# A sliding-window copy: batch 0 moved from the staged to the direct path, with larger transfers on two of the three DMA rings

## The chip, the cores and the metric

The kernel runs on one core of a Trainium2 chip. The metric is the device time of one execution in microseconds (us); three runs of the kernel before are shown, and their median is the time before. One execution was also taken by the hardware profiler; its span (first to last instruction on the core) is a little shorter than its time.

## The reference: what is computed

The input `x` has 32 batches of 4096 rows of 256 float32 values. Each batch is cut into windows of 64 rows that start every 32 rows, so that each window overlaps the next by half, and there are 127 windows in a batch. Nothing is calculated; the work is a copy in which nearly every input row is written twice.

```python
n_windows = (length - window_size) // stride + 1     # 127
for i in range(n_windows):
    start = i * stride
    result[:, i] = x[:, start:start + window_size].copy()
```

A block is 32 rows of 256 values, 32 KB (32,768 bytes). A batch is 128 blocks, 4.19 MB. A window is two neighbouring blocks, 64 KB, and the output of a batch is 127 windows, 8.32 MB. All outputs together are 266.3 MB.

## The kernel before, in words

All work is done by DMAs. There is no matmul and no arithmetic, and the engines' instruction streams only issue transfers and wait for semaphores. Two kinds of path carry the data.

**Staged batches.** Twelve batches (1, 4, 7, ... 28, then 30, then 0; line 134) are loaded into on-chip memory (SBUF) by `Copier.load` (L59, L60) as a tile of 128 partitions, one block each, and written out twice by `Copier.store` (L65, L72): once with every block as the first half of its window (`half` 0), and once as the second half (`half` 1). Each DMA of 128 rows is cut into pieces of 16,384 bytes. A staged batch so costs 4.19 MB in and 8.39 MB out. `Staging.run` (L109) issues these on ScalarE's ring (`ring_s`, called ACT here): six loads, the stores of these six, the next six loads, and the stores of those. There are six buffers, so a second-round load waits until its buffer is stored (L91).

A store of all 128 blocks writes one row too many: block 127 as a first half lies in window 127, which does not exist and is window 0 of the next batch; block 0 as a second half lies in the last window of the batch before. These spilled rows are wrong there, and the true windows have to be written after them. The last staged batch alone is stored without spilling, by four DMAs of 112, 15, 15 and 112 rows (L97 to L100), which count on a semaphore of their own, `last`. `spilled` (L139) is the list of the other eleven.

**Direct batches.** The other 20 batches are copied from DRAM to DRAM by `Copier.windows` (L42, L48), on SyncE's ring (`ring_d`, called SP). Each batch is seven jobs of 16 windows (1 MB each, L171 to L182). A job is issued either as one DMA of whole windows, or split into two DMAs of half-windows, one for each half. Either way its data go in pieces of 32,768 bytes. Which jobs are split is set by a fraction that is counted up at L174: `share += 12 if at < loads else 9`, and a job is split when the sum reaches 12. `turns` adds 4 for a split job and 3 for a whole one, which are the packets that one DMA engine handles for it: two data packets and one completion packet for each of its DMAs. `at` compares the turns so far with those of six loads (`6 * 17`) and their stores (`6 * 34`), so it tells whether the ACT ring is in a round of loads or of stores.

**Remainders.** Seven jobs of 16 cover 112 of 127 windows. The 15 windows left of each direct batch are those that lie beside a staged neighbour where there is one (`first`, L144, and `rest_parts`, L147), so that they are written after the neighbour's spilled rows. Batch 29 has a spilling neighbour on both sides and gets two parts, of 8 and 7 windows. The remainders are issued on GpSimd's software ring (`ring_r`, called POOL, L186 to L192). It first waits for `near`, which the third-last direct job sets (`todo == 3`, L179 and L182), and then, batch by batch in the order of their last staged neighbour, for that neighbour's stores (`wait_stored`, L190, with the wait itself at L107). The remainders take their piece size in turn from `PIECES`: 32,768 and 16,384.

At the end SP waits for the direct jobs, the remainders and the last staged batch (L193 to L195).

The queues in the profile are: q1 = SP's ring, q10 = ACT's ring, q0 = the software ring of POOL. All three feed the same 16 DMA engines.

Of the kernel before, what the change touches and what calls it, by code (L numbers as in the profile page):

```python
# [6 lines left out]


DIRECT, IN, OUT = 32768, 16384, 16384
PIECES = (32768, 16384,)  # L10


class Copier:
# [105 lines left out]
@with_exitstack  # L119
def kernel(  # L120
    ctx: ExitStack,
    tc: tile.TileContext,
    x: bass.AP,
    window_size: bass.AP,
    stride: bass.AP,
    out: bass.AP,
):
    nc = tc.nc
    W, S = int(window_size), int(stride)
    B, L, D = x.shape  # L130
    n_win = (L - W) // S + 1
    assert out.shape == (B, n_win, W, D)
    c = Copier(nc, tc, x, out, B, L, D, W, S, n_win)
    staged = [*range(1, B - 3, 3), B - 2, 0]
    direct = [b for b in range(B) if b not in staged]
    pool = ctx.enter_context(tc.tile_pool(name="xb", bufs=1))
    st = Staging(c, pool, x.dtype, staged, 6)
    ring_d, ring_s = nc.sync, nc.scalar
    spilled = staged[:-1]  # L139

    waits = {b: [g for g, n in enumerate(spilled) if abs(n - b) == 1] for b in direct}
    per, loads, stores = 6, 6 * 17, 34

    def first(b):  # L144
        return 0 if b - 1 not in spilled else 8 if len(waits[b]) == 2 else 15

    def rest_parts(b):  # L147
        if len(waits[b]) == 2:
            return [(0, 8), (120, 7)]
        return [(0 if b - 1 in spilled else 112, 15)]  # L150

    soft = tc.alloc_semaphore("soft")
    soft_total = 0

    near = tc.alloc_semaphore("near")

    def mark(dma):
        dma.then_inc(near, 16)

    def count_soft(dma):  # L160
        nonlocal soft_total
        dma.then_inc(soft, 16)
        soft_total += 16

    with tc.tile_critical():  # L165
        st.run(ring_s)

        turns = share = 0
        rests = []
        todo = 7 * len(direct)  # L170
        for b in direct:  # L171
            for j in range(7):
                at = turns % (loads + per * stores)
                share += 12 if at < loads else 9  # L174
                if share >= 12:
                    share -= 12
                    turns += 4
                    c.windows(ring_d, b, first(b) + 16 * j, 16, 0)
                    c.windows(ring_d, b, first(b) + 16 * j, 16, 1, count=mark if todo == 3 else None)  # L179
                else:  # L180
                    turns += 3
                    c.windows(ring_d, b, first(b) + 16 * j, 16, count=mark if todo == 3 else None)  # L182
                todo -= 1
            rests.append(b)

        ring_r = nc.gpsimd  # L186
        ring_r.wait_ge(near, 16)
        for i, b in enumerate(sorted(rests, key=lambda b: max(waits[b], default=0))):
            for g in waits[b]:
                st.wait_stored(ring_r, g)  # L190
            for w, n in rest_parts(b):
                c.windows(ring_r, b, w, n, None, PIECES[i % 2], count_soft)  # L192
        ring_d.wait_ge(c.done, c.total)  # L193
        ring_d.wait_ge(soft, soft_total)
        ring_d.wait_ge(c.last, c.last_total)  # L195
# [35 lines left out]
```

## Time and profile before

| What | Value |
|---|---|
| Time, median of 3 runs (lowest to highest) | 752.54 us (752.53 to 753.82) |
| Profiled execution: time | 752.54 us |
| Profiled execution: span | 750.8 us |
| Bytes moved by the DMA engines | 317.43 MB, 423 GB/s over the span |
| ACT ring (q10) | 9,818 packets, 150.93 MB |
| SP ring (q1) | 8,608 packets, 146.82 MB |
| Software ring (q0) | 1,328 packets, 19.66 MB |
| DMAs on SP | 236 of 512 KB, 22 of 1,024 KB |
| DMAs on ACT | 12 loads and 22 stores of 4,096 KB; 2 stores of 3,584 KB and 2 of 480 KB |
| DMAs on POOL | 19 of 960 KB, 1 of 512 KB, 1 of 448 KB |

A queue's line gives its packets (short completion packets included), its bytes, and the time that its packets took as a share of 16 engines over the span: 47.4% on q10 means 0.474 x 16 x 750.8 us of engine time. A DMA from SBUF to DRAM or back touches the DRAM once for each byte, a DMA from DRAM to DRAM twice, so the DRAM's traffic is larger than what the engines move.

### The profile page before, as it was taken

What the parts mean: (1) busy time and instruction counts of PE and PEld (TensorE: products, weight loads), DVE (VectorE), ACT (ScalarE), POOL (GpSimd) and SP (SyncE); (2) the same over time, 40 slices, a digit from 0 to 9 for tenths busy, and PEclk for the clock granted to TensorE, in tenths of its full rate; (3) what the DMA queues carried; (4) which work ended last, traced back from release to release, by engine and by line L of the source; (5) the groups of instructions that cost most, each with busy time, mean ns of one, the idle gap of its engine ahead of it and who ended that gap; (6) DMA issues with size and microseconds to landing.
All of it is one profiled execution on the core that took longest, in us unless ns stands there. A gap on an engine that the chain in (4) does not pass through costs nothing.

```text
span 750.8 us, 372 instructions
## 1 busy us (share of the span) xinstructions
POOL 12.2 (2%) x25
## 2 busy tenths in 40 slices
POOL 0000000000000000000000000000000000410000
DMA  9999999999999999999999999999999999999995
GB/s 377 433 428 433 432 431 424 430 428 433 437 423 433 433 430 443 423 432 429 423 425 431 430 433 433 432 433 429 428 436 432 429 431 436 430 427 430 417 394 220
DMA packets 19756, 317.43 MB, mean 423 GB/s; under 512 B 5162, under 2 KB 5162, under 8 KB 5162
## 3 DMA queue, kind: packets, MB, share of 16 engines
q10 hardware_dynamic: 9818, 150.93, 47.4%
q1 hardware_dynamic: 8608, 146.82, 45.6%
q0 software_dynamic: 1328, 19.66, 6.1%
q14 instruction: 2, 0.02, 0.0%
HBM read 216.79 MB, written 267.06 MB: 644 GB/s over the span
## 4 chain that ended last, share of the span: by engine, by line
another core or an unknown queue 92%; POOL 2%; issue 0%; POOLq 0%; SPq 0%
POOL out_dram L48 2%; POOLq L107 0%; POOLq L226 0%; SPq L165 0%
## 5 line engine op out<-in xcount | busy, mean ns | idle before, releaser
L48 POOL DMA_DIRECT2D out_dram<-in_x_dram x21 | 12.0, 577 | 692.7 <-DMA out_dram<-in_x_dram 648.5
L212 POOL MEMSET const-float32-0.0<- 128x1 f32 x1 | 0.1, 98 | 0.2 <-issue 0.2
L212 POOL MEMSET const-bfloat16-1.0<- 128x1 bf16 x1 | 0.1, 101 | 0.0
L212 POOL MEMSET const-float32-1.0<- 128x1 f32 x1 | 0.1, 98 | 0.0
L212 POOL MEMSET const-uint8-127<- 128x1 uint8 x1 | 0.1, 98 | 0.0
## 6 DMA issues: line engine op xcount, KB each, us to landing
out_dram<-in_x_dram SPq DMA_DIRECT2D x236, 512.0 KB, 87.5
out_dram<-xb ACTq DMA_DIRECT2D x22, 4096.0 KB, 128.6
xb<-in_x_dram ACTq DMA_DIRECT2D x12, 4096.0 KB, 119.9
out_dram<-in_x_dram SPq DMA_DIRECT2D x22, 1024.0 KB, 89.2
out_dram<-in_x_dram POOLq DMA_DIRECT2D x19, 960.0 KB, 44.3
out_dram<-xb ACTq DMA_DIRECT2D x2, 3584.0 KB, 112.3
out_dram<-xb ACTq DMA_DIRECT2D x2, 480.0 KB, 96.2
out_dram<-in_x_dram POOLq DMA_DIRECT2D x1, 512.0 KB, 36.6
```

Of the source, the lines that this page charges most:

```text
L48: q.dma_start(out=self.oap((b * self.nw + w0) * 2 * blk + off, [[2 * blk, n], [1, size]]), in_=bass.AP(self.x.tensor, self.x.offset + (b * ...
L212: nc = _bacc.Bacc("TRN2", target_bir_lowering=False, num_devices=1)
```

## The change

Batch 0 is taken off the staged list, and nothing is put in its place: 11 batches are staged and 21 are direct. Batch 30 is now the last staged one, so it is stored by the four DMAs that don't spill, and the neighbours 29 and 31 no longer wait for it; batch 29's remainder becomes one part of 15 windows. The share of split jobs becomes 9 of 12 in rounds of loads and 3 of 12 in rounds of stores, from 12 and 9. All remainders use pieces of 32,768 bytes.

```diff
-PIECES = (32768, 16384,)
+PIECES = (32768,)
...
-    staged = [*range(1, B - 3, 3), B - 2, 0]
+    staged = [*range(1, B - 3, 3), B - 2]
     direct = [b for b in range(B) if b not in staged]
...
                 at = turns % (loads + per * stores)
-                share += 12 if at < loads else 9
+                share += 9 if at < loads else 3
                 if share >= 12:
...
             for w, n in rest_parts(b):
-                c.windows(ring_r, b, w, n, None, PIECES[i % 2], count_soft)
+                c.windows(ring_r, b, w, n, None, PIECES[i % 1], count_soft)
```

In DMAs: ACT issues 11 loads instead of 12, 20 full stores instead of 22, and the same four of the last batch. SP issues 64 split jobs and 83 whole ones (128 DMAs of 512 KB and 83 of 1,024 KB) instead of 118 and 22. POOL issues 21 DMAs of 15 windows, each as 15 rows of two pieces, instead of 21 of three sizes.

## Prediction

> **What bounds the kernel now.** I read the page's strip of 40 slices first, then its queues, then the same queues in stretches.
>
> ```profile
> span 750.8 us, 372 instructions
> ...
> DMA  9999999999999999999999999999999999999995
> GB/s 377 433 428 433 432 431 424 430 428 433 437 423 433 433 430 443 423 432 429 423 425 431 430 433 433 432 433 429 428 436 432 429 431 436 430 427 430 417 394 220
> DMA packets 19756, 317.43 MB, mean 423 GB/s; under 512 B 5162, under 2 KB 5162, under 8 KB 5162
> ...
> q10 hardware_dynamic: 9818, 150.93, 47.4%
> q1 hardware_dynamic: 8608, 146.82, 45.6%
> q0 software_dynamic: 1328, 19.66, 6.1%
> ...
> HBM read 216.79 MB, written 267.06 MB: 644 GB/s over the span
> ```
>
> All 16 DMA engines are busy in every slice but the last, and the shares of the three rings add to 99.1%. The rate stands near 430 GB/s from the second slice to the third-last. So nothing but the engines' own time bounds the kernel: a wait that leaves the rings full costs nothing, and a byte taken off the rings is time taken off. (The chain of waits says only "another core or an unknown queue 92%", which is this same DMA time.)
>
> Is it the engines, or the DRAM behind them? A stretch in which rings have other shares tells.
>
> ```profile
> DMA packets 2664, 43.33 MB, mean 433 GB/s; under 512 B 717, under 2 KB 717, under 8 KB 717
> ## 3 DMA queue, kind: packets, MB, share of 16 engines
> q1 hardware_dynamic: 1335, 22.87, 53.4%
> q10 hardware_dynamic: 1328, 20.45, 47.7%
> ```
>
> These are 100 to 200 us. DRAM traffic there is 2 x 22.87 + 20.45 = 66.2 MB in 100 us, 662 GB/s, at 433 GB/s moved. In 660 to 700 us (8.62 MB on q10, 8.60 on q0, by the same view) it is 646 GB/s, at 431 moved. What the engines move doesn't fall when the DRAM carries more. The engines are the bound, as far as this trace reaches, which is 662. The same view shows **the turn order**: 1,335 packets of q1 and 1,328 of q10. An engine serves two full rings in turn, one packet each, and a completion packet takes a turn like any other. So the ring with larger packets gets more of the time.
>
> **Price of a byte on each ring.** Engine time by bytes, from the queue lines:
> - q10: 0.474 x 16 x 750.8 = 5,694 engine-us for 150.93 MB: 26.5 GB/s for one engine, 618 ns for a 16 KB packet with its share of completions.
> - q1: 0.456 x 16 x 750.8 = 5,478 for 146.82 MB: 26.8 GB/s, 1,223 ns for 32 KB.
> - q0: 0.061 x 16 x 750.8 = 733 for 19.66 MB: 26.8 GB/s.
>
> A byte from DRAM to DRAM so costs no more than one between SBUF and DRAM. A staged batch moves 4.19 + 8.39 MB, a direct one 8.32 MB.
>
> **The change, part by part.**
>
> 1. *Batch 0 leaves the staged list.* q10 after: 11 loads x 4.194 + 20 stores x 4.194 + the last batch's 254 rows, 8.32 = 138.35 MB, 12.58 less. At 26.5 GB/s that is -474.7 engine-us. q1 after: 147 jobs x 1.0486 = 154.14 MB, +7.34, or +273.9 at 26.8. q0: 21 x 15 windows = 20.64 MB, +0.98, or +36.6. Sum -164.2 engine-us, over 16 engines **-10.3 us**. Second way: the total falls by 4.295 MB (317.43 to 313.13); the stretches from 100 to 700 us moved 258.5 MB, 430.9 GB/s, so **-10.0 us**. I take -10.1.
>
> 2. *Fewer split jobs on SP.* Bytes and packet sizes stay; one DMA fewer for each job that is now whole. The completions on an engine go from 258 to 211. They are tiny (the price in 1 holds them): 0 to -0.5 us. What this does change is the turns: SP's ring needs 64 x 4 + 83 x 3 = 505 on each engine, from 118 x 4 + 22 x 3 = 538, so it carries more bytes in fewer turns.
>
> 3. *Larger pieces on the software ring.* The price of a byte was equal on q0 and q1, so 0 by itself; ten of 20 remainders had 16 KB pieces, and at q10's price against q1's (1%) of 9.8 MB the bound is 0 to 0.2 us. In turns: ten DMAs of 3 and ten of 5, 80 x 15/16 = 75 for an engine, become 21 x 3 x 15/16 = 59.
>
> 4. *Do the rings still end together?* ACT's turns: a 128-row DMA is 16 packets and a completion, 17; the last four stores are 15 + 3 + 3 + 15 = 36. Before 12 x 17 + 22 x 17 + 36 = 614, after 31 x 17 + 36 = 563. When SP is through, ACT has 614 - 538 = 76 turns left before, against 75 of q0; after, 563 - 505 = 58 against 59. The balance is kept. It also matters little: if one ring dries up, the engine gives all its time to the other.
>
> 5. *POOL's waits.* `near` is set two jobs before SP's end. Check of the count on before: a turn of q1 is 5,478/8,608 = 636 ns, of q10 5,694/9,818 = 580; 538 x 1.216 = 654, and with 2 us of start SP ends at 656, two split jobs (8 turns, 9.7 us) after `near`: 647.
>
> ```profile
> 648.99 9.74 POOL L48 DMA_DIRECT2D out_dram<-in_x_dram  x17 [648.54 <-DMA out_dram<-in_x_dram]
> 663.00 0.58 POOL L48 DMA_DIRECT2D out_dram<-in_x_dram  x1 [4.27 <-DMA out_dram<-xb]
> 703.44 1.70 POOL L48 DMA_DIRECT2D out_dram<-in_x_dram  x3 [39.86 <-DMA out_dram<-xb]
> ```
>
> The timeline has POOL going at 648.5, and the last wait, for a spilling batch's stores, over at 703.4; the count gives 76 - 36 = 40 turns of (580 + 611) after 656, 704. So it can be trusted for after: SP's turn is 154.14 MB / 26.8 / 16 = 359.5 us / 505 = 712 ns; it ends at 505 x 1.292 + 2 = 654, `near` lands about 646. Batch 28, the last that spills, is stored 22 turns of (580 + 812) later, at 685. Until then POOL holds back two remainders (27 and 29); behind them in POOL's stream is only the end. The 19 others keep q0 full for 57 turns, to about 654 + 57 x 1.39 = 733. The wait has 48 us of cover. If the cover were gone, two remainders would run alone after the rest, 2 x 2.4 us and a start of about 5.
>
> 6. *Loads in the second round.* Five loads instead of six lie ahead of the first store that waits for one of them. While that wait lasts ACT's ring holds four loads of 17 turns, over 80 us of work, so it doesn't dry up: 0.
>
> 7. *The tail.* At the end the engines don't stop together.
>
> ```profile
> DMA  9949939829658466134031222020010000000000
> ...
> DMA packets 269, 2.95 MB, mean 184 GB/s; under 512 B 117, under 2 KB 117, under 8 KB 117
> ...
> q0 software_dynamic: 216, 2.31, 33.9%
> q10 hardware_dynamic: 53, 0.64, 9.6%
> ```
>
> In 735 to 751 us the 2.95 MB would need 6.8 us at full rate; the last packets end in the 31st of 40 slices, near 747.5. About 3.5 us are the end of the program, and about 5 are spread between the engines. The strip falls from 700 us on (417, 394), while the last staged batch's 112- and 15-row stores run: the packet records show q10 packets of 1 to 4 us there instead of 0.61, 38 engine-us over the usual in all, 2.4 us for each engine, unevenly. These four stores remain, for batch 30. I take their cost and the spread as unchanged: 0. The bounds are -5 us (no spread) and +5 (twice the spread).
>
> **Sum:** 750.8 - 10.1 = 740.7 us of span. The profiled execution took 752.5, 1.7 over its span, and equals the median of the runs. **Forecast 742.4 us**, -1.35%.
>
> **A rule that speaks against it.** The change trades 4.19 MB of loads for direct reads: DRAM traffic goes from 483.9 to 487.9 MB. Measured is 644 GB/s over the span and 662 in a stretch. The Trainium skill (HBM Reference, Specifications (TRN2)) gives about 716 GB/s for a domain and about 358 as one core's part. By the 358 the added 4.06 MB would be an estimated +11 us, the wrong way; but the 644 of this trace already refutes it for this run. By the 716, 487.9 MB would be an estimated 681 us, which still leaves the engines as the bound.
>
> **Rivals.**
> - *The DRAM becomes the bound; slower.* In rounds of stores SP's ring will get 750/(750 + 580) = 56% of an engine's time (three whole jobs to a split one: 13 turns, 8 packets of 1,223 ns), so the DRAM carries 1.56 x 431 = 674 GB/s, 2% over what the trace shows. For it: at 369 us the records have all 16 engines start a direct packet within 1.3 us, and these take 1.31 to 1.54 us instead of 1.21. Against: only some 1% of direct packets were so stretched, and the engines then fall out of step. Price: held at 644 GB/s of DRAM, 487.9 MB need 758 us of span, **759 us**. It decides when the DRAM can't hold 650 GB/s in the mean, or when about 49 of an engine's 294 direct packets take 0.2 us more (49 x 0.208 = 10).
> - *Partly so:* stretched packets as in 350 to 400 us (10.6 engine-us over the usual in 50 us) all through would be 740 x 10.6 / 50 / 16 = 9.8 us: **752 us**, no change.
> - *The tail eats half:* the larger last packets and another hand of uneven stores double the spread, +5: **747.5 us**. The records give single engines up to 5 us more than the mean there, which speaks for some luck in it either way.
> - *The change doesn't keep the rings balanced* (POOL late, a ring dry): 5 to 10 us lost, **750 us**. Against it stand the counts of 4 and 5.
>
> **Chances.** Forecast within a few us 0.74, tail 0.10, balance lost 0.04, partly DRAM-bound 0.05, DRAM-bound 0.07. What a measurement can tell from no change is 0.2%, 1.5 us. Faster (under 751.0) 0.87, same 0.05, slower 0.08. Range: down to 738.5 (a spread smaller by 4 us), up to 748 (the tail's 747.5); what lies out of it is about 0.17.
>
> **What would show it.** q10 at 138.35 MB, q1 at 154.14, q0 at 20.64; the rate near 430 in the slices; 26.5 to 26.8 GB/s of each ring's engine time. POOL waiting for `near` until about 646 and for the last stores until about 685. A rate under 428 in the middle slices, with q1's price over 1,223 ns, is the DRAM. A rate of 430 with more than 16 us of falling strip is the tail.

## The result, and the profile after

The changed kernel took **745.38 us** (median of 4 runs, 745.27 to 745.96) against 752.6 us of the kernel before on the same chip: ratio 0.990, 95% interval 0.9885 to 0.9919. The forecast was 742.4, the range 738.5 to 748. So the direction held, the bytes and the balance of the rings came out nearly as counted, and about 3 us of the 10 are missing.

These are the lines of the page of the changed kernel that answer to those of before: the strip, the queues, and the DRAM's traffic.

```profile
span 743.5 us, 321 instructions
...
DMA  8999999999999999999999999999999999999995
GB/s 368 431 430 427 426 436 436 423 440 420 431 432 425 427 438 420 435 427 421 439 423 408 431 434 432 434 424 433 427 437 429 430 425 437 421 435 432 414 420 191
DMA packets 18092, 313.16 MB, mean 421 GB/s; under 512 B 4312, under 2 KB 4312, under 8 KB 4312
...
q1 hardware_dynamic: 8080, 154.15, 48.5%
q10 hardware_dynamic: 9002, 138.35, 43.8%
q0 software_dynamic: 1008, 20.65, 6.8%
...
HBM read 220.92 MB, written 266.99 MB: 656 GB/s over the span
```

The bytes are those of the count: 138.35, 154.15 and 20.65 MB. The three shares still add to 99.1%, so the engines were as full as before. Engine time by ring, by the prediction's own sum (one engine-us is one engine busy for 1 us; 16 of them are 1 us of the kernel):

| Ring | predicted, engine-us | measured | price of a byte, one engine |
|---|---|---|---|
| q10 | 5,694 - 475 = 5,219 | 0.438 x 16 x 743.5 = 5,210 | 26.55 GB/s (before 26.5) |
| q1 | 5,478 + 274 = 5,752 | 0.485 x 16 x 743.5 = 5,770 | 26.7 (26.8) |
| q0 | 733 + 37 = 770 | 0.068 x 16 x 743.5 = 809 | 25.5 (26.8) |
| sum | 11,741 | 11,789 | |

Against before's 11,905 that is -116 engine-us, or -7.3 us on 16 engines, and the span fell by just this, from 750.8 to 743.5. So the loss isn't in engines that stood idle: the same bytes took 48 engine-us more than by the old prices, 3.0 us, and most of it stands on q0. (A share is rounded to 0.1%, 12 engine-us; the packet records give 5,212, 5,775 and 806 for the three rings.)

The timeline of POOL shows the waits near where the count had put them (646 and 685 us were predicted; the first is 5 us late).

```profile
651.85 11.05 POOL L48 DMA_DIRECT2D out_dram<-in_x_dram  x19 [651.41 <-DMA out_dram<-in_x_dram]
685.76 1.16 POOL L48 DMA_DIRECT2D out_dram<-in_x_dram  x2 [22.86 <-DMA out_dram<-xb]
```

Where the bytes became dearer is seen in stretches. Here is 200 to 400 us, nearly all a round of stores, first of the kernel before, then of the changed one (packets, MB and share of the engines by queue).

```profile
DMA packets 5246, 85.94 MB, mean 430 GB/s; under 512 B 1392, under 2 KB 1392, under 8 KB 1392
...
q1 hardware_dynamic: 2623, 45.59, 53.3%
q10 hardware_dynamic: 2623, 40.35, 47.2%
```

```profile
DMA packets 4817, 85.63 MB, mean 428 GB/s; under 512 B 1072, under 2 KB 1072, under 8 KB 1072
...
q1 hardware_dynamic: 2409, 48.53, 57.1%
q10 hardware_dynamic: 2408, 37.09, 43.5%
```

Turns still go one to one, and q1 has the larger share that was meant. The DRAM's traffic rose from 2 x 45.59 + 40.35 = 131.5 MB (658 GB/s) to 134.2 (671 GB/s), and the engines moved 0.3 MB less in spite of fewer completions. The end shows it plainly. This is the changed kernel from 720 to 735 us, when ACT's ring has nearly run out:

```profile
DMA packets 290, 5.42 MB, mean 362 GB/s; under 512 B 104, under 2 KB 104, under 8 KB 104
...
q0 software_dynamic: 234, 4.75, 85.6%
q10 hardware_dynamic: 56, 0.67, 12.3%
```

The engines are 97.9% busy and move only 362 GB/s; the DRAM carries 2 x 4.75 + 0.67 = 10.17 MB in 15 us, 678 GB/s. That led to the **theory**: the DRAM holds no more than some 660 to 680 GB/s, and the change asks for more wherever direct packets take more than their mean share. The main **rival**: the engines are the only bound, and the 3 us are luck in the tail.

The packet records give sizes, as engine time over the usual 0.611 us for 16 KB and 1.213 us for 32 KB. For q1 it grew from 9 to 39 engine-us, for q0 from 2 to 38; for q10 it grew from 19 to 39 up to 650 us and fell from 39 to 9 after that. By time, all rings together: from 28 to 78 up to 650 us, in the rounds, and from 41 to 47 after that. So the rounds cost 3 us, and what q0 lost at the end ACT's ring nearly gave back.

### The profile page after: what moved, and what is told of

The parts are those of the page before. It is cut to its first block, busy times and chain, and to the rows that moved or that the text cites. A ratio compares the mean times of both kernels' runs of the same rounds, so it can differ in the third digit from the quotient of the medians.

```text
span 743.5 us, 321 instructions
## 1 busy us (share of the span) xinstructions
POOL 12.4 (2%) x25
## 3 DMA queue, kind: packets, MB, share of 16 engines
q1 hardware_dynamic: 8080, 154.15, 48.5%
q10 hardware_dynamic: 9002, 138.35, 43.8%
q0 software_dynamic: 1008, 20.65, 6.8%
## 4 chain that ended last, share of the span: by engine, by line
another core or an unknown queue 91%; POOL 2%; issue 0%; POOLq 0%; SPq 0%
POOL out_dram L48 2%; POOLq L226 0%; SPq L165 0%; POOLq L107 0%
```

## The experiments

They ran in three groups of four, on three chips, each beside the kernel before on its own chip (755.97, 755.46 and 752.46 us). Times are to be compared within a group, or by ratios.

### All batches direct

```diff
-    staged = [*range(1, B - 3, 3), B - 2]
+    staged = []
...
-    st = Staging(c, pool, x.dtype, staged, 6)
+    st = Staging(c, pool, x.dtype, staged, 1)
...
-        st.run(ring_s)
...
-                share += 9 if at < loads else 3
+                share += 0
...
-        ring_d.wait_ge(c.last, c.last_total)
```

> No batch is staged; all 32 go from DRAM to DRAM, whole jobs on SP's ring, the remainders on the software ring. Theory (the DRAM holds no more than about 680 GB/s; in the changed kernel 720 to 735 us moved 4.75 MB on q0 and 0.67 on q10, 678 GB/s of DRAM traffic at 362 GB/s moved): 266.3 MB are read and written, 532.7 MB at 680 are 783 us, so 780 to 795 us, about 340 GB/s moved, and direct packets of 32 KB near 1.5 us. Rival (the engines are the only bound, and the missing 3 us are luck in the tail): 266.3 MB at 431 GB/s are 618 us, so 625 to 640 us and packets of 1.21 us.

Measured: **816.8 us**, in one run. The page of this kernel:

```profile
span 815.0 us, 307 instructions
...
DMA packets 12290, 266.37 MB, mean 327 GB/s; under 512 B 4160, under 2 KB 4160, under 8 KB 4160
...
q1 hardware_dynamic: 10752, 234.90, 87.3%
q0 software_dynamic: 1536, 31.46, 11.8%
...
HBM read 266.34 MB, written 266.34 MB: 654 GB/s over the span
```

The engines are 99.1% busy and move 327 GB/s. 0.873 x 16 x 815.0 us for 234.90 MB are 1.59 us for each 32 KB, instead of 1.22. The rival (625 to 640 us) is out. There is a second limit behind the engines. The theory's 780 to 795 us was missed too, since it had put the limit at 680 GB/s; the kernel stood at 654 on this chip. The kernel before, at 644 to 662, lay just under it, which its own trace could not tell.

### The batch moved, the turns left as they were

```diff
-PIECES = (32768,)
+PIECES = (32768, 16384,)
...
-                share += 9 if at < loads else 3
+                share += 12 if at < loads else 9
...
-                c.windows(ring_r, b, w, n, None, PIECES[i % 1], count_soft)
+                c.windows(ring_r, b, w, n, None, PIECES[i % 2], count_soft)
```

> Batch 0 is direct as in the changed kernel, but the split shares (12 and 9 of 12) and the two piece sizes are those of before. SP then needs 564 turns against ACT's 563, so the remainders are left over and run alone. Theory (DRAM limit near 680 GB/s): no stretch in the middle (-3 us), but 20.65 MB alone at 340 GB/s are 61 us instead of 48, and a few us to start: 752 to 757 us. Rival (engines only; turns decide nothing as long as a ring has work): 744 to 747 us.

Measured: **757.6 us**, ratio 1.002 (1.0003 to 1.004), where the kernel before took 756.0. That is just above the theory's 752 to 757, and far from the rival's 744 to 747. So taking batch 0 off the staged list alone gains nothing. Its stretch from 690 to 740 us says why:

```profile
DMA packets 1082, 16.63 MB, mean 333 GB/s; under 512 B 325, under 2 KB 325, under 8 KB 325
...
q0 software_dynamic: 1080, 16.63, 100.1%
```

The remainders are alone on full engines, at 333 GB/s, 665 of the DRAM. The prediction held that a ring that dries up costs nothing, since the engine gives its time to the other. That is not so when the other is a ring of direct copies. Without the change of shares and pieces the batch brings no gain.

### One split share for all rounds

```diff
-                share += 9 if at < loads else 3
+                share += 4
```

> The changed kernel with 4 of 12 jobs split in every round, instead of 9 in rounds of loads and 3 in rounds of stores. SP needs 490 turns instead of 505; its share of engine time is then 734/(734+580) = 56% everywhere, the mean of direct bytes over the whole kernel, and more of ACT's ring is left beside the remainders. Theory (the DRAM is over its limit in the rounds of stores and in the tail, where direct bytes are over the mean): 742 to 744 us. Rival (luck in the tail): 745.4 within 0.7 us. Second rival (whole jobs stretch packets by their addresses, not by the rate): 745 to 747 us, as more jobs are whole.

Measured: **754.5 us**, ratio 0.998 (0.9964 to 0.9999), on the chip with 756.0 before. The changed kernel was not in that group, so this alone told nothing of the difference; the two ran again side by side.

> The changed kernel once more, beside the three below on one chip, as the four kernels before ran on a chip where the kernel before took 756 us instead of 752.6. Theory (DRAM limit, 655 to 666 GB/s in the kernel that copies all from DRAM to DRAM): the gain depends on how much the DRAM of the chip holds; where the kernel before is slower than 752.6, the changed kernel, with 4 MB more of DRAM traffic in less time, loses more: ratio 0.990 to 1.000. Rival (engines only): ratio 0.990 within 0.002 on any chip.

> The kernel with 4 of 12 jobs split in every round, beside the changed one. Theory: 1 to 3 us less than the changed kernel on the same chip, as no stretch asks for much more than the mean from the DRAM and the remainders don't end alone. Rival (luck in the tail): equal within 0.7 us.

Measured: the changed kernel **752.4 us**, ratio 0.9955 (0.9931 to 0.9978); the even share **754.7**, ratio 0.999 (0.9964 to 1.0017). Two things follow. The gain was not the same on this chip: here it is 0.45%, and by the records the engine time over the usual is 14.9 us for each engine in this run, 7.8 in the first. And the theory failed on the even share: it should have won 1 to 3 us and lost 2.2. The first 100 us (5 to 105), a round of loads, show where; first the changed kernel on that chip, then the even share:

```profile
DMA packets 2568, 42.72 MB, mean 427 GB/s; under 512 B 656, under 2 KB 656, under 8 KB 656
...
q1 hardware_dynamic: 1279, 22.78, 53.5%
q10 hardware_dynamic: 1289, 19.94, 47.3%
```

```profile
DMA packets 2367, 41.93 MB, mean 419 GB/s; under 512 B 526, under 2 KB 526, under 8 KB 526
...
q1 hardware_dynamic: 1180, 23.53, 55.5%
q10 hardware_dynamic: 1187, 18.40, 45.2%
```

With two points more for direct copies the rate falls from 427 to 419 GB/s, and the DRAM's traffic is the same: 2 x 22.78 + 19.94 = 65.5 MB and 2 x 23.53 + 18.40 = 65.5 MB in 100 us, 655 GB/s. So on this chip the round of loads is at the limit already with the changed kernel's share, and a larger share only slows it. What the even share was to win beside the stores is little: by the same view 150 to 350 us moved 84.7 MB in both. At the end it did win: the records have q0 at 21 engine-us over the usual instead of 43. But q1 and q10 together rose from 196 to 254, so that 37 are left, 2.3 us, which is the loss. The theory's mistake was to look for the limit in the rounds of stores alone.

The second rival, that whole jobs stretch packets by their addresses, can be asked of the records, as each packet starts where the one before it on its engine ends, so that a job's packets can be told apart. In the kernel before, the 692 packets found of whole jobs between 10 and 640 us are 3.8 ns over the usual in the mean, and without the one moment at 369 us 0.2 ns. In the changed kernel 2,510 of them are 12.5 ns over, and those of split jobs 3.4; on the chip of this experiment split jobs' packets are 10.5 over with the changed kernel, and 16.7 with the even share. So the form alone doesn't stretch a packet. But whole jobs in a row are also what asks most of the DRAM, and no run has the one without the other.

### One batch more off the staged list

```diff
-    staged = [*range(1, B - 3, 3), B - 2]
+    staged = [*range(1, B - 3, 3)]
...
-                share += 9 if at < loads else 3
+                share += 0
```

> One more batch, 30, goes from staged to direct; all jobs are whole. The engines move 308.8 MB, the DRAM 492 MB. Theory (DRAM limit): the 4.3 MB less bring nothing, as 492 MB at 670 to 680 GB/s are 724 to 734 us, with 11 us of start and end 736 to 747 us, and direct packets are stretched all through. Rival (engines only): 716.6 us at 430.9 GB/s, with 14.1 of start and tail and 1.7 over the span 732 us.

Measured: **758.4 us**, ratio 1.004 (1.0025 to 1.0059). The rival's 732 us is out. The theory's range of 736 to 747 is missed as well: it had 670 to 680 GB/s in it. A sum made after the result, by the limit that the all-direct kernel shows on this chip, has 492 MB at 654 to 660, 745 to 752 us, and with 13 us of start, tail and time over the span 758 to 765. The 4.3 MB less on the engines brought nothing. By the records the packets are 508 engine-us over the usual, 31.7 us for each engine, and 229 of the 508 stand on ACT's ring. So transfers between SBUF and DRAM are stretched as well as copies within the DRAM: the limit is one that both meet.

### The turns changed, the batch left staged

```diff
-PIECES = (32768, 16384,)
+PIECES = (32768,)
...
-                share += 12 if at < loads else 9
+                share += 9 if at < loads else 3
...
-                c.windows(ring_r, b, w, n, None, PIECES[i % 2], count_soft)
+                c.windows(ring_r, b, w, n, None, PIECES[i % 1], count_soft)
```

(against the kernel before)

> Twelve staged batches as before, with the new split shares and the new piece size only; the bytes are those of before. SP needs 483 turns against ACT's 614, so it ends early, and about 75 turns of ACT's ring are left alone after the remainders. Theory (DRAM limit): the first 600 us ask for 674 GB/s instead of 655 and are stretched, and nothing is given back at the end where the engines are the bound: 2 to 5 us more than before. Rival (engines only): as before within 1.5 us.

Measured: four runs of **767.8, 774.1, 779.5 and 781.8 us**; the ratio 1.020 (1.011 to 1.029) is that of the two shorter ones, 12 to 19 us over the kernel before. Slower was expected, but 2 to 5 us of it. The view from 710 to 745 us of its profile, which is that of the longest run:

```profile
DMA packets 802, 12.26 MB, mean 350 GB/s; under 512 B 84, under 2 KB 84, under 8 KB 84
...
q10 hardware_dynamic: 754, 11.27, 95.7%
```

ACT's ring is nearly alone, reads from SBUF, and asks for 2 x 0.98 + 11.27 = 13.2 MB of DRAM in 35 us, 378 GB/s. Neither limit explains 350 GB/s, falling to some 200 at the end. By the bytes that ACT's ring has left (8.32 MB from 727 us on), the last staged batch's four stores run where the rate falls: the engines move 431 GB/s from 710 to 727 us, and 274 from 727 to 745. How much of this end the shorter runs share is not shown.

### The pieces alone

```diff
-PIECES = (32768, 16384,)
+PIECES = (32768,)
...
-                c.windows(ring_r, b, w, n, None, PIECES[i % 2], count_soft)
+                c.windows(ring_r, b, w, n, None, PIECES[i % 1], count_soft)
```

(against the kernel before)

> The kernel before with pieces of 32,768 bytes in all remainders. Their turns fall from 75 to 56 for an engine, so some 19 turns of ACT's ring (12 us) are left alone at the end. Theory (the price of a byte is the same for both sizes, and the DRAM is under its limit in the tail on the average): as before within 1.5 us. Rival (the 37 engine-us by which packets of ACT's last stores were stretched in the kernel before, and only 9 in the changed one, come from the 16 KB pieces beside them): 1.5 to 2.5 us less than before, and that stretch gone.

Measured: **753.5 us**, ratio 0.997 (0.9948 to 0.9994). That is 2.0 us less, the time of the rival; but its cause isn't there. Packets of ACT's ring after 650 us were over the usual by 38 engine-us, as in the profile of the kernel before (39). So 16 KB pieces beside them are not what stretches ACT's last stores. Where the 2 us come from is not shown, as the kernel before was not profiled on that chip, and the interval reaches from 0.5 to 3.9.

### Stores, loads and jobs by themselves

```python
phase("a", loads())
phase("b", stores(128))
phase("c", stores(112))
phase("d", stores(15, p0=112))
phase("e", loads(), [0] * 34)          # 34 whole jobs on SP beside six loads
phase("f", stores(128), [0] * 34)
phase("g", loads(), [1] * 25)          # 25 split jobs
phase("h", stores(128), [1] * 25)
```

> Not the whole work: eight stretches one after the other, each begun when the one before has ended, which write only parts of the output: six loads; six stores of 128 rows (25.2 MB); six of 112 rows (22.0 MB); six of 15 rows (2.9 MB); six loads beside 34 whole jobs; six stores beside 34 whole jobs (60.8 MB each); six loads beside 25 split jobs; six stores beside 25 split jobs (51.4 MB each). Theory: stores of 112 and 15 rows are slow by their form, whatever runs beside them: 128 rows near 430 GB/s (59 us), 112 rows 250 to 330 GB/s (67 to 88 us), 15 rows under 250; and loads beside whole jobs are stretched more (145 us and over) than stores beside whole jobs (141 to 144), and both more than beside split jobs (119 to 122). Rival for the stores: no form costs more for a byte, the stretch at the end comes from what runs beside: 22.0 MB in 51 to 53 us. Rival for the rounds: loads and stores beside whole jobs alike within 1 us.

The profile of this kernel in three stretches, one inside each of the phases b, c and d (65 to 120, 130 to 190 and 206 to 230 us):

```profile
DMA packets 1520, 23.59 MB, mean 429 GB/s; under 512 B 80, under 2 KB 80, under 8 KB 80
```

```profile
DMA packets 1226, 18.69 MB, mean 312 GB/s; under 512 B 85, under 2 KB 85, under 8 KB 85
```

```profile
DMA packets 214, 2.24 MB, mean 94 GB/s; under 512 B 77, under 2 KB 77, under 8 KB 77
```

The same 16 KB pieces, from the same tiles, go at 429 GB/s in stores of 128 rows, at 312 in stores of 112 rows (283 over the whole phase) and at 94 in stores of 15. By the records a packet takes 0.62, 0.81 and 2.36 us in the mean of a phase; the phases, first packet to last, take 59, 78 and 31 us. The rival (22.0 MB in 51 to 53 us) is out: these stores are slow by their form.

For the rounds, the phases take 148.2 us (loads beside whole jobs), 146.0 (stores beside whole jobs), and 120.5 and 120.9 beside split jobs. 60.8 MB at 430.9 GB/s are 141 us, 51.4 MB are 119. So whole jobs are stretched, beside loads more than beside stores, and split jobs hardly; the stores beside whole jobs came out 2 us over the 141 to 144 that were expected. Inside the two phases with whole jobs the DRAM carried 661 GB/s beside loads and 672 beside stores:

```profile
DMA packets 2913, 54.25 MB, mean 417 GB/s; under 512 B 568, under 2 KB 568, under 8 KB 568
...
q1 hardware_dynamic: 1454, 31.66, 57.5%
q10 hardware_dynamic: 1459, 22.59, 42.9%
```

```profile
DMA packets 2852, 53.04 MB, mean 424 GB/s; under 512 B 560, under 2 KB 560, under 8 KB 560
...
q1 hardware_dynamic: 1425, 30.97, 58.9%
q10 hardware_dynamic: 1427, 22.07, 41.7%
```

These are 245 to 375 us (2 x 31.66 + 22.59 = 85.9 MB in 130 us) and 395 to 520 us (84.0 MB in 125 us). In these two phases the DRAM carried a little less beside loads.

### Split shares moved further apart, and the pieces undone

```diff
-                share += 9 if at < loads else 3
+                share += 12 if at < loads else 2
```

> The changed kernel, as the measure for the two below on the same chip. Theory: ratio to the kernel before between 0.990 and 0.997, with direct and staged packets both stretched where the gain is small. Rival: 0.990 within 0.002.

> The changed kernel with all jobs split in rounds of loads and 2 of 12 in rounds of stores; SP needs 508 turns, 3 more. Theory (loads beside whole jobs are what is stretched first; an even share in all rounds had cost 2.2 us more than the changed kernel): 0.5 to 2 us less than the changed kernel, and the stretch from 0 to 150 and 400 to 500 us falls. Rival (only the mean of direct bytes matters): equal within 0.7 us.

Measured: the changed kernel **745.8 us**, ratio 0.990 (0.9872 to 0.9926), as at first. The shares moved apart: **747.6**, ratio 0.993 (0.9902 to 0.9952), 1.9 us more, where 0.5 to 2 less were expected: a miss. By the records q1's time over the usual fell in the first 100 us, from 1.4 to 0.4 engine-us, and rose from 100 to 400 us, from 32 to 54. What is taken off the loads comes back, and more, beside the stores. The even share on the other side was also worse, so of the three tried 9 and 3 are the best.

The last kernel, on the same chip, has the two piece sizes of before:

```diff
-PIECES = (32768,)
+PIECES = (32768, 16384,)
...
-                c.windows(ring_r, b, w, n, None, PIECES[i % 1], count_soft)
+                c.windows(ring_r, b, w, n, None, PIECES[i % 2], count_soft)
```

> The changed kernel with the two piece sizes of before for the remainders. They then need 78 turns for an engine, against 58 left of ACT's ring, so about 20 turns (12 us) of them run alone, where the DRAM allows 330 GB/s instead of 430. Theory: 2 to 4 us more than the changed kernel. Rival (the piece size is worth nothing, as a byte has one price): equal within 0.7 us.

Measured: **750.3 us**, ratio 0.996 (0.9938 to 0.9981), 4.5 us more than the changed kernel. The theory had 2 to 4: right in sign, a little short in size. From 720 to 735 us its remainders are alone:

```profile
DMA packets 342, 5.16 MB, mean 344 GB/s; under 512 B 105, under 2 KB 105, under 8 KB 105
...
q0 software_dynamic: 335, 5.13, 99.9%
```

In the same stretch of the first profile of the changed kernel they had 85.6% of the engines, at 362 GB/s. So the larger pieces are worth more than half of the gain, and the turns that they save are at least part of it.

By the ratios, none of these kernels beats the changed one.

## Why the prediction was right, and where it was off

- **What bounds the kernel** (the engines): right, and the reading "as far as this trace reaches, which is 662" was the right limit to put on it. The second limit begins about there. Naming the DRAM at 650 to 674 GB/s as the rival was right; giving its partial form 0.05 was too little. What happened is that form, at a third of its size; at its full size, 752 us, it would have lain outside the range.
- **Steps 1 to 3** (-10.1 us from bytes at old prices): the term that was mis-sized. By the records, the work without any stretch fell by 171 engine-us, 10.7 us; the stretch grew from 70 to 125, which gives 3.4 back. That direct traffic meets such a limit is shown by the all-direct kernel and by the remainders alone (333 GB/s), and the rounds of the changed kernel, at 671 GB/s, stand at the same height. Whether the limit sits in the DRAM itself or on the way to it, no run tells. It isn't luck in the tail: the changed kernel came back to 0.990 in the third group, and to 0.9955 on a chip where more packets are stretched.
- **Step 3** ("0 by itself" for the pieces): wrong by what it left to step 4. It counted the turns that the pieces save, and step 4 gave them no price; undoing the pieces cost 4.5 us.
- **Step 4** ("it also matters little" if a ring dries up): wrong in both directions. Remainders left alone run at 333 GB/s; stores of 112 rows left alone run at 312, of 15 rows at 94. The balance of the rings, which the count got nearly right, is what the gain hangs on. It was off by a few turns: q0 has 1,008 packets, 63 for an engine and not 59 (378 are completions, 18 for each DMA, where the count had 15), against ACT's 58. So ACT's ring ended first, and from 720 to 735 us q0 was already almost alone. For the kernel before it is 83 and not 75.
- **Step 5** (POOL's waits): right within 5 us, 651 and 686 against 646 and 685.
- **Step 6** (five loads in the second round): nothing in the profile speaks against it; the engines are full there.
- **Step 7** (the tail unchanged): its sum was nearly so, its parts were not. ACT's stretched packets after 650 us fell from 39 to 9 engine-us, and q0 took 36 more. Why ACT's fell so far is not settled. The time that ACT's ring has beside q0 doesn't explain it: on one chip, with 43 to 45% of the engines from 660 to 735 us, the pieces-alone kernel has 38 engine-us, and with 42 to 43% the even share has 16. In the profiles at hand it is 38 and more in the three kernels that store batch 0 last, and 9 to 23 in the nine others with staged batches; no run parts the batch from the rest.
- **The rule that speaks against it** (the 716 GB/s for a domain of the Trainium skill, HBM Reference, Specifications (TRN2)): these runs got less from copies within the DRAM. The all-direct kernel stood at 654 with its engines 99.1% busy. By an estimate from the page's 716 its 532.7 MB would have taken 744 us; they took 815 of span.

## What to carry to other kernels

Before you trade staged bytes for direct ones, count both sides: what the DMA engines move and what the DRAM carries, and measure the second limit with a kernel made of that traffic alone. When rings share engines turn by turn, packet sizes set who ends last; count the turns of each ring and see that no ring of one costly kind is left alone. A profile that shows full engines does not show that a packet takes its usual time: divide the engine time by the bytes, ring by ring and stretch by stretch.

## What the runs showed of the hardware

- Copies from DRAM to DRAM alone: 327 GB/s moved, 654 GB/s of DRAM traffic, 1.59 us for 32 KB on one engine, against 1.22 us when half of the time goes to SBUF transfers.
- Stores from SBUF by rows, alone: 128 rows 429 GB/s, 112 rows 312, 15 rows 94. The Trainium skill (DMA: Bandwidth & Descriptors, The descriptor swizzle) has four neighbouring partitions on one port, and a transfer to 128 partitions so dealt that each engine writes one port. If the same ports serve the reads of a store, and 15 neighbouring rows go to 15 engines one by one, four engines share a port, by estimate 4 x 0.611 = 2.44 us for 16 KB; the 2.36 us measured agree. The runs show the times only, not the ports.
- The same kernel can differ between chips: the changed one took 745.4, 745.8 and 752.4 us in the three groups where it ran, with its runs 0.7 to 3.5 us apart within one. The medians of the one before lie between 752.5 and 756.0, but in the three groups of experiments its own runs are 6 to 8 us apart.
- One engine ends behind the others: in the changed kernel's last stretch, from 735 us, the engines move 0.16 MB in 17 packets: five 32 KB pieces, of which the last four run one after the other until 740.1 us. Why this engine is late was not tried.
